# Where fifteen column sums are scaled, and how the second-last row is split: the tail of a row-sum kernel

## The chip, the cores and the metric

The kernel runs on one core of a Trainium2 chip. The metric is the device time of one execution in microseconds (us), the median of several runs; lower is better. Besides the timed runs there is one execution that the hardware profiler recorded, and all durations below are from it.

## The reference

The input is 32 x 512 x 1024 numbers in float32 (64 MiB). Every row of 1024 is summed and divided by 1024:

```python
def reference(x: np.ndarray, divisor: float) -> np.ndarray:
    return (np.sum(x, axis=-1) / divisor).astype(np.float32)
```

So 67 MB are read and 64 KB are written; there are 16384 row sums.

## The kernel before

The 16384 rows are laid over 128 partitions, 128 rows in each. A partition's first 112 rows (the main part) and its last 16 rows (the last part) lie in different stretches of the input and of the output, so that the main part's results can be stored while the last part is still being read. A "column" below is one of these rows seen from the result tiles: `res` holds 112 columns of finished sums, `q` and `fin` 16 each.

**The loads.** All loads are issued by SyncE (SP), in program order, on one DMA queue. The main part comes in pieces of 2, 14 (seven times) and 12 rows per partition, into three rotating buffers `t`. The last part comes as 8 rows (a fourth use of those buffers), then 4 and 2 rows in tiles of their own, then one row (`row`, lines 172 to 176), and then the very last row in three pieces: `pa` (columns 0 to 447), `pb` (448 to 703) and `pc` (704 to 1023), lines 180 to 186. Rows 8 + 4 + 2 are 14, so `j` is 14 at line 172: `row` is column 14 of the last part, and the three pieces are column 15.

**The sums.** Of each piece VectorE (DVE) sums most rows with one `reduce_sum` (line 153); in the pieces at the end ScalarE (ACT) sums some rows, one ACTIVATE each with an accumulator that a second instruction reads out (line 147). The single row `row` is split between the two engines: DVE sums its first 768 elements into `q[:, 14]` (line 176), ACT sums the other 256, already multiplied by 1/1024, into `r[:, 14]` (line 175). `r` is set to zero by a GpSimd (POOL) memset at the start (line 139), because line 194 reads fifteen columns of it.

**The tail.** ACT sums `pa` into an extra column of `pc` (line 192), DVE sums `pb` into a second extra column (line 193). Line 194 is one DVE instruction that makes `fin[:, 0:15]` as `q * scale + r`. Line 198 is one DVE instruction that multiplies `pc`, with its two extra columns, by 1/1024 and accumulates the result into `fin[:, 15]`; this too is followed by an instruction that reads the accumulator. Line 201 stores `fin`. Earlier, at line 189, POOL multiplies the 112 columns of `res` by 1/1024, and line 190 stores them.

**What sets the order.** The engines work through the program in its order; semaphores are set by the tile framework, by the regions of a tile that are written and read. Three functions edit the finished program. `start_loads_at_once` puts the first loads ahead of the start barrier. `latest_wait_first` orders an instruction's waits where it has several: the first stays on the instruction, the others go to small semaphore instructions ahead of it. `close_while_storing` moves the last store (line 201) behind SP's closing drain (line 232 in the profile), so that the other engines' closing barrier runs while the store is under way. SP's closing waits thus stand ahead of the last store: one for each load that is still out, for the landing of the store of `res`, and for the last work of POOL and ACT. The store itself then waits for DVE alone, and the program's end waits for the store's landing (line 88).

Of the kernel before, what the change touches and what calls it, by code (L numbers as in the profile page):

```python
# [9 lines left out]
F32 = mybir.dt.float32  # L10
ADD = mybir.AluOpType.add
MULT = mybir.AluOpType.mult
# [55 lines left out]
def close_while_storing(nc, landed):  # L68


    body, end = nc.main_func.blocks[1], nc.main_func.blocks[-1]
    store = [i for i in body.instructions if i.engine == SP and type(i).__name__ == "InstDMACopy"][-1]
    (lane,) = store.sync_info.on_update
    drain = end.instructions[0]
    assert drain.engine == SP and type(drain).__name__ == "InstDrain"
    needs = {w.id: w for w in drain.sync_info.on_wait}
    assert needs[lane.id].wait_value > lane.update_value
    needs[lane.id] = dataclasses.replace(
        needs[lane.id], wait_value=needs[lane.id].wait_value - lane.update_value
    )  # L80

    (done,) = [w for w in store.sync_info.on_wait if w.ant_name.startswith("DVE_")]
    assert needs[done.id].wait_value == done.wait_value
    del needs[done.id]
    own = dict(sync_type="semaphore", id=landed.num, ant_name=landed.name)
    add = mybir.SyncUpdate(update_mode="sem-add-imm", update_value=16, **own)
    sub = mybir.SyncUpdate(update_mode="sem-sub-imm", update_value=16, **own)
    last = nc.sync.wait_ge(landed, 16).ins
    assert nc.main_func.blocks[-1].instructions[-1].name == last.name
    body.instructions = [i for i in body.instructions if i.name != store.name]  # L90
    end.instructions = [
        with_sync(drain, on_wait=tuple(needs.values())),
        with_sync(store, on_wait=(done,), on_update=(add,)),
        *end.instructions[1:-1],
        with_sync(last, on_update=(sub,)),
    ]


@with_exitstack
def kernel(  # L100
    ctx: ExitStack,
    tc: tile.TileContext,
    x: bass.AP,
    divisor: float,
    out: bass.AP,
):
    nc = tc.nc
    landed = nc.alloc_semaphore("landed")
    nc.at_finalize(start_loads_at_once)
    nc.at_finalize(latest_wait_first)  # L110
    nc.at_finalize(lambda nc: close_while_storing(nc, landed))
    xf = x.flatten_outer_dims()
    N, D = xf.shape
    P = nc.NUM_PARTITIONS
    scale = 1.0 / float(divisor)
    J = N // P
    assert J * P == N


    L = 16  # L120
    M = J - L
    x_main = bass.AP(tensor=x.tensor, offset=0, ap=[[M * D, P], [D, M], [1, D]])
    x_last = bass.AP(tensor=x.tensor, offset=P * M * D, ap=[[L * D, P], [D, L], [1, D]])
    o_main = bass.AP(tensor=out.tensor, offset=0, ap=[[M, P], [1, M]])
    o_last = bass.AP(tensor=out.tensor, offset=P * M, ap=[[L, P], [1, L]])


    main = [(2, 0)] + [(14, 0)] * 6 + [(14, 4), (12, 5)]
    last = [(8, 4), (4, 2), (2, 1)]
    assert sum(n for n, _ in main) == M and sum(n for n, _ in last) == L - 2  # L130
    bulk = ctx.enter_context(tc.tile_pool(name="bulk", bufs=3))
    one = ctx.enter_context(tc.tile_pool(name="one", bufs=1))
    psum = ctx.enter_context(tc.tile_pool(name="junk", bufs=4, space=bass.MemoryType.PSUM))

    res = one.tile([P, M], F32, name="res")
    fin = one.tile([P, L], F32, name="fin")
    q = one.tile([P, L], F32, name="q")
    r = one.tile([P, L], F32, name="r")
    nc.gpsimd.memset(r, 0.0)  # L139

    def load(dst, src):
        tc.keep_in_program_order(nc.sync.dma_start(out=dst, in_=src))  # L142

    def act_sum(dst, src, by=1.0):
        n = src.shape[-1]
        junk = psum.tile([P, D], F32, name="junk")
        nc.scalar.activation(junk[:, :n], src, COPY, scale=by, accum_out=dst)  # L147

    def sums(dst, t, rows, on_act):
        d = rows - on_act  # L150
        for i in range(d, rows):
            act_sum(dst[:, i : i + 1], t[:, i, :])
        nc.vector.reduce_sum(out=dst[:, :d], in_=t[:, :d, :], axis=AX)  # L153

    j = 0
    for rows, on_act in main:
        t = bulk.tile([P, 14, D], F32, name="t")
        load(t[:, :rows, :], x_main[:, j : j + rows, :])
        sums(res[:, j : j + rows], t, rows, on_act)
        j += rows  # L160
    j = 0
    for rows, on_act in last:
        if rows == 8:
            t = bulk.tile([P, 14, D], F32, name="t")[:, :8, :]
        else:
            t = one.tile([P, rows, D], F32, name=f"t{rows}")
        load(t, x_last[:, j : j + rows, :])
        sums(q[:, j : j + rows], t, rows, on_act)
        j += rows


    c = 768
    row = one.tile([P, D], F32, name="row")
    load(row, x_last[:, j, :])
    act_sum(r[:, j : j + 1], row[:, c:], by=scale)
    nc.vector.reduce_sum(out=q[:, j : j + 1], in_=row[:, :c], axis=AX)  # L176

    a, b = 448, 704  # L180
    pa = one.tile([P, a], F32, name="pa")
    pb = one.tile([P, b - a], F32, name="pb")
    pc = one.tile([P, D - b + 2], F32, name="pc")
    load(pa, x_last[:, L - 1, :a])
    load(pb, x_last[:, L - 1, a:b])
    load(pc[:, : D - b], x_last[:, L - 1, b:])


    nc.gpsimd.tensor_scalar_mul(out=res, in0=res, scalar1=scale)  # L189
    tc.keep_in_program_order(nc.sync.dma_start(out=o_main, in_=res))  # L190

    act_sum(pc[:, D - b : D - b + 1], pa)
    nc.vector.reduce_sum(out=pc[:, D - b + 1 :], in_=pb, axis=AX)  # L193
    nc.vector.scalar_tensor_tensor(  # L194
        out=fin[:, : L - 1], in0=q[:, : L - 1], scalar=scale, in1=r[:, : L - 1], op0=MULT, op1=ADD
    )
    scaled = one.tile([P, D - b + 2], F32, name="scaled")
    nc.vector.tensor_scalar(  # L198
        out=scaled, in0=pc, scalar1=scale, scalar2=0.0, op0=MULT, op1=ADD, accum_out=fin[:, L - 1 :]
    )  # L200
    tc.keep_in_program_order(nc.sync.dma_start(out=o_last, in_=fin))
# [35 lines left out]
```

## Time and profile before

| | us |
|---|---|
| median of 4 runs | 161.35 (161.31 to 161.41) |
| the profiled execution: its own time | 161.32 |
| its span, first to last instruction | 159.8 |
| DVE busy | 121.1 (76%) |
| ACT busy | 19.6 (12%) |
| POOL busy | 0.8 |
| DMA: 67.18 MB | mean 420 GB/s over the span |

The span leaves out some 1.5 us of the profiled execution's time that lies around the program's instructions. The busy time of an engine is a mean over the whole span; the tail that the change touches is the last 4 us, and it is read from the views in order of time. "Landing" is when a DMA's last piece has signalled its semaphore.

The rows of the operations that the change touches: the memset of `r` took 112 ns, the DVE sum of `row` 954 ns for 768 columns, ACT's sum of the other 256 columns 388 ns and 187 ns to read the accumulator, line 194 on DVE 174 ns, and POOL's scaling of `res` (112 columns) 493 ns.

### The profile page before, as it was taken

Reading aid. Unit: us, or ns where it says so; the run is one execution under the profiler, and the core shown is the slowest. Engines: PE = TensorE matmul, PEld = TensorE weight load, DVE = VectorE, ACT = ScalarE, POOL = GpSimd, SP = SyncE. Lnnn points to the kernel's source line nnn. Section 1 sums busy time; section 2 is a strip of 40 time slices with the busy share of each in tenths; the row PEclk is TensorE's granted clock in tenths of the full one; section 3 lists DMA queues with packets and bytes.
Section 4 is the critical chain, followed back from the end, with each engine's and each line's share of the span. In section 5 each row is a group of like instructions: output and inputs, shape, how many; then the busy total and the mean of one; then the engine's idle time right before and its main releaser. Section 6 shows DMA issues by size and latency. Waiting matters only on the chain.

```text
span 159.8 us, 139 instructions
## 1 busy us (share of the span) xinstructions
DVE 121.1 (76%) x17; ACT 19.6 (12%) x37; POOL 0.8 (0%) x6
## 2 busy tenths in 40 slices
DVE  0500059995999599978999599959995996494985
ACT  3000000000000000000000000000000900480973
POOL 0000000000000000000000000000000000001000
DMA  7999999978999999969999999969999999899993
GB/s 248 474 459 459 459 459 459 445 316 388 459 459 459 459 459 459 445 302 402 459 459 459 459 459 459 445 273 431 459 459 427 394 468 517 361 427 390 402 410 128
DMA packets 2592, 67.18 MB, mean 420 GB/s; under 512 B 544, under 2 KB 928, under 8 KB 1056
## 3 DMA queue, kind: packets, MB, share of 16 engines
q1 hardware_dynamic: 2592, 67.18, 98.0%
HBM read 67.11 MB, written 0.07 MB: 420 GB/s over the span
## 4 chain that ended last, share of the span: by engine, by line
DMA 76%; DVE 22%; SPq 0%; issue 0%; DVEq 0%
DMA t<-in_x_dram 76%; DVE res L153 20%; DVE q L153 1%; DVE q L176 1%; SPq L142 0%; DVE scaled L198 0%; DVE pc L193 0%; DVE fin L194 0%; DVEq L198 0%; DVEq L232 0%
## 5 line engine op out<-in xcount | busy, mean ns | idle before, releaser
L153 DVE TENSOR_REDUCE res<-t 128x14 f32<-128x14336 f32 (+3 forms) x9 | 111.2, 12360 | 34.4 <-DMA t<-in_x_dram 34.4
L147 ACT ACTIVATE junk<-t 128x1024 f32<-128x1024 f32 x16 | 16.2, 1012 | 135.9 <-DMA t<-in_x_dram 135.9
L153 DVE TENSOR_REDUCE q<-t 128x4 f32<-128x4096 f32 (+2 forms) x3 | 7.9, 2642 | 2.7 <-DMA t<-in_x_dram 2.5
L147 ACT ACTIVATION_READ_ACCUMULATOR junk<-t 128x1 f32 x16 | 3.0, 187 | 0.0
L147 ACT ACT_TABLE_LOAD x1 | 1.3, 1283 | 1.7 <-PEq L218 1.7
L189 POOL TENSOR_SCALAR res<-res 128x112 f32<-128x112 f32 x1 | 0.5, 493 | 143.9 <-DVE res L153 143.9
L176 DVE TENSOR_REDUCE q<-row 128x1 f32<-128x768 f32 x1 | 1.0, 954 | 0.0
L198 DVE TENSOR_SCALAR_CACHE_REDUCE scaled<-pc 128x322 f32<-128x322 f32 x1 | 0.5, 489 | 0.1
L147 ACT ACTIVATE junk<-pa 128x448 f32<-128x448 f32 x1 | 0.5, 548 | 0.0
L193 DVE TENSOR_REDUCE pc<-pb 128x1 f32<-128x256 f32 x1 | 0.4, 411 | 0.0
L147 ACT ACTIVATE junk<-row 128x256 f32<-128x256 f32 x1 | 0.4, 388 | 0.1
L194 DVE SCALAR_TENSOR_TENSOR fin<-q,r 128x15 f32<-128x15 f32 x1 | 0.2, 174 | 0.0
L147 ACT ACTIVATION_READ_ACCUMULATOR junk<-row 128x1 f32 x1 | 0.2, 187 | 0.0
L147 ACT ACTIVATION_READ_ACCUMULATOR junk<-pa 128x1 f32 x1 | 0.2, 187 | 0.0
L139 POOL MEMSET r<- 128x16 f32 x1 | 0.1, 112 | 1.3 <-POOLq L218 1.3
L218 POOL MEMSET const-uint8-127<- 128x1 uint8 x1 | 0.1, 102 | 0.0
L218 POOL MEMSET const-bfloat16-1.0<- 128x1 bf16 x1 | 0.1, 101 | 0.0
L218 POOL MEMSET const-float32-0.0<- 128x1 f32 x1 | 0.1, 99 | 0.2 <-issue 0.2
L218 POOL MEMSET const-float32-1.0<- 128x1 f32 x1 | 0.1, 100 | 0.0
L198 DVE DVE_READ_ACCUMULATOR scaled<-pc 128x1 f32 x1 | 0.1, 81 | 0.0
## 6 DMA issues: line engine op xcount, KB each, us to landing
t<-in_x_dram SPq DMA_DIRECT2D x7, 7168.0 KB, 35.7
t<-in_x_dram SPq DMA_DIRECT2D x1, 6144.0 KB, 33.3
t<-in_x_dram SPq DMA_DIRECT2D x1, 4096.0 KB, 26.0
t<-in_x_dram SPq DMA_DIRECT2D x2, 1024.0 KB, 18.7
t<-in_x_dram SPq DMA_DIRECT2D x1, 2048.0 KB, 30.5
row<-in_x_dram SPq DMA_DIRECT2D x1, 512.0 KB, 33.2
pa<-in_x_dram SPq DMA_DIRECT2D x1, 224.0 KB, 33.3
pc<-in_x_dram SPq DMA_DIRECT2D x1, 160.0 KB, 33.1
```

The costliest lines, as they stand in the source:

```text
L139: nc.gpsimd.memset(r, 0.0)
L147: nc.scalar.activation(junk[:, :n], src, COPY, scale=by, accum_out=dst)
L153: nc.vector.reduce_sum(out=dst[:, :d], in_=t[:, :d, :], axis=AX)
L176: nc.vector.reduce_sum(out=q[:, j : j + 1], in_=row[:, :c], axis=AX)
L189: nc.gpsimd.tensor_scalar_mul(out=res, in0=res, scalar1=scale)
L193: nc.vector.reduce_sum(out=pc[:, D - b + 1 :], in_=pb, axis=AX)
L194: nc.vector.scalar_tensor_tensor(out=fin[:, : L - 1], in0=q[:, : L - 1], scalar=scale, in1=r[:, : L - 1], op0=MULT, op1=ADD)
L198: nc.vector.tensor_scalar(out=scaled, in0=pc, scalar1=scale, scalar2=0.0, op0=MULT, op1=ADD, accum_out=fin[:, L - 1 :])
L218: nc = _bacc.Bacc("TRN2", target_bir_lowering=False, num_devices=1)
```

## The change

The scaling of columns 0 to 14 of `fin` goes from one DVE instruction to two POOL instructions: one scales the fourteen columns of `q`, the other makes column 14 as `q * scale + r`, with `r` as a value for each partition. `r` is now one column wide (a view of a tile of 16 columns, as wide as the tile was before), so it needs no zeroing, and the memset goes. `row` is split 704 to 320 between DVE and ACT in place of 768 to 256. The pieces of the very last row (448, 256 and 320 columns) are the same before and after, and no tile changes its size.

```diff
     res = one.tile([P, M], F32, name="res")
     fin = one.tile([P, L], F32, name="fin")
     q = one.tile([P, L], F32, name="q")
-    r = one.tile([P, L], F32, name="r")
-    nc.gpsimd.memset(r, 0.0)
+
+    r = one.tile([P, 16], F32, name="r")[:, :1]
...
-    c = 768
+    c = 704
     row = one.tile([P, D], F32, name="row")
     load(row, x_last[:, j, :])
-    act_sum(r[:, j : j + 1], row[:, c:], by=scale)
+    act_sum(r, row[:, c:], by=scale)
     nc.vector.reduce_sum(out=q[:, j : j + 1], in_=row[:, :c], axis=AX)
...
     act_sum(pc[:, D - b : D - b + 1], pa)
     nc.vector.reduce_sum(out=pc[:, D - b + 1 :], in_=pb, axis=AX)
-    nc.vector.scalar_tensor_tensor(
-        out=fin[:, : L - 1], in0=q[:, : L - 1], scalar=scale, in1=r[:, : L - 1], op0=MULT, op1=ADD
+    nc.gpsimd.tensor_scalar_mul(out=fin[:, :j], in0=q[:, :j], scalar1=scale)
+    nc.gpsimd.tensor_scalar(
+        out=fin[:, j : j + 1], in0=q[:, j : j + 1], scalar1=scale, scalar2=r, op0=MULT, op1=ADD
     )
```

## The prediction

> **What bounds the kernel now.** I read first the page's chain of work that ended last, by line.
>
> ```profile
> DMA t<-in_x_dram 76%; DVE res L153 20%; DVE q L153 1%; DVE q L176 1%; SPq L142 0%; DVE scaled L198 0%; DVE pc L193 0%; DVE fin L194 0%; DVEq L198 0%; DVEq L232 0%
> ```
>
> The loads carry it. The change touches no load, so it can act only behind the last of them: on L176, L194, L193 and L198, some 2 us in all. Next, the end of the same chain in order of time (start, duration, what).
>
> ```profile
> 156.19 0.96 DVE q L176
> 157.16 0.02 issue
> 157.18 0.17 DVE fin L194
> 157.35 0.34 DVE pc L193
> 157.69 0.04 DVEq L198
> 157.73 0.06 issue
> 157.79 0.49 DVE scaled L198
> ```
>
> From 156.19 on, DVE works without a gap that matters, and its end releases the store. Two of these pieces change: L176 gets shorter, L194 goes. Then the timeline, for what lies beside them (start, duration, engine, line).
>
> ```profile
> 145.69 0.49 POOL L189 TENSOR_SCALAR res<-res 128x112 f32<-128x112 f32 x1 [143.85 <-DVE res L153]
> ...
> 156.19 0.39 ACT L147 ACTIVATE junk<-row 128x256 f32<-128x256 f32 x1
> ...
> 156.74 0.55 ACT L147 ACTIVATE junk<-pa 128x448 f32<-128x448 f32 x1
> 157.18 0.17 DVE L194 SCALAR_TENSOR_TENSOR fin<-q,r 128x15 f32<-128x15 f32 x1
> 157.22 0.19 ACT L147 ACTIVATION_READ_ACCUMULATOR junk<-pa 128x1 f32 x1
> 157.27 0.41 DVE L193 TENSOR_REDUCE pc<-pb 128x1 f32<-128x256 f32 x1
> ```
>
> POOL has been idle since 146.18. ACT has its last sum at 157.41. L193 starts at 157.27, before L194 has ended (157.18 + 0.17 = 157.35): independent DVE instructions overlap by 0.08. Last, SP's own waits and the DMAs' landings, because SP must pass its closing waits before it may issue the last store.
>
> ```profile
> SPq L232 <- DMA out_dram<-res: 0.6, 1, 0.6
> ...
> SPq L201 <- DVE scaled L198: 0.5, 1, 0.5
> ```
>
> ```profile
> row<-in_x_dram SPq DMA_DIRECT2D x1, 512.0 KB, 33.2
> pa<-in_x_dram SPq DMA_DIRECT2D x1, 224.0 KB, 33.3
> pc<-in_x_dram SPq DMA_DIRECT2D x1, 160.0 KB, 33.1
> pb<-in_x_dram SPq DMA_DIRECT2D x1, 128.0 KB, 33.1
> out_dram<-res SPq DMA_DIRECT2D x1, 56.0 KB, 11.5
> out_dram<-fin SPq DMA_DIRECT2D x1, 8.0 KB, 1.4
> ```
>
> With the issue times of the timeline (122.94, 123.42, 124.37, 123.89, 146.21, 158.32) the landings are: `row` 156.1, `pa` 156.7, `pc` 157.5, `pb` 157.0, the store of `res` 157.7, the last store 159.7. The span ends with that landing. SP is free of the `res` store at 157.7 and then stands 0.5 for DVE: that is the most that a faster tail can give before this store binds.
>
> **The change part by part.**
>
> *The memset of `r` goes* (112 ns at 1.72): POOL's next work is at 145.69. Worth nothing; 143 us of idle POOL hide it.
>
> *DVE's part of `row`, 768 to 704 columns.* Two DVE sums of one row give the slope: (954 - 411) ns / (768 - 256) = 1.06 ns per column, so 64 columns are 68 ns and L176 takes 0.89. It starts at 156.19 as before, on the landing of `row` (ACT starts on it in the same moment), and ends at 157.08.
>
> *ACT's part, 256 to 320 columns.* Slope (548 - 388) / (448 - 256) = 0.83 ns, so 53 ns more. The cover: ACT's sum of `pa` starts at 156.74 because `pa` lands at 156.7. The readout of `row` moves from 156.51 to 156.56; earlier ACTIVATEs start 0.09 behind such a readout's start (153.49 to 153.58), so ACT is ready by 156.65. Cost nothing; if the cover were gone, 0.05 on an engine that still has 0.1 to spare, see below.
>
> *L194 leaves DVE.* Its start to the start of L193 is 157.18 to 157.27, 0.09; before it, DVE waited 0.03 to 0.04 for its own sum to be written, which L193 needn't. So L193 can start at the end of L176 plus the old gap, 157.11, or, with the overlap of 0.08 that the pair L194, L193 shows, at 157.00. There `pb` stops it: it lands at 157.0 and starts follow a landing by 0.02 (154.94 to 154.96), so about 157.05. L193 starts at 157.05 to 157.11 in place of 157.27: 0.16 to 0.22 earlier.
>
> *What is late next for L198.* It starts 0.11 behind the end of L193 (157.68 to 157.79), now at 157.57 to 157.63. Its other inputs: ACT's sum of `pa`, 157.41 + the same 0.11 = 157.52, and `pc`, 157.5 + 0.02. Both are earlier, by 0.05 to 0.1. So the whole 0.16 to 0.22 arrives, and no more than 0.27 could.
>
> *Two instructions come on POOL, and with them a new wait of SP.* Both are the operation of L189 (TENSOR_SCALAR), with 14 columns and with one. Nothing shows them this small, or with a scalar read from memory: below, POOL's own 128x1 memsets take 0.10; above, L189 takes 0.49 for 112 columns. I take 0.49 for both, the only row of the operation. The first needs the 14 columns of `q`, ready at 154.96 + 1.22 = 156.18; POOL starts 0.09 behind DVE (145.60 to 145.69), so it runs 156.27 to 156.76, beside L176. The second needs L176, 157.08, and ACT's 320 columns, 156.75: it runs 157.17 to 157.66 (157.27 at the lower bound). Nothing is queued behind it on POOL but the closing drain, which nobody needs before SP's store has been issued. SP sees POOL 0.03 later (146.18 to 146.21), at 157.69: that is while SP still stands for the `res` store. DVE releases the last store at 158.32 - 0.2 = 158.12. The cover is thus 0.43 beyond the 0.49; I price the pair at nothing.
>
> The Trainium skill, "GPSIMD Engine Reference", section "When to use GPSIMD", speaks against such a move: elementwise work belongs on VectorE, GpSimd taking about twice as long. By that each would take 2 x 0.17 = 0.35 and still be hidden, so rule and trace disagree on the merit, not on the duration: the rule prices an engine, the chain prices a place in time.
>
> *The sum.* 159.76 - 0.20 in the span (the page's 159.8; the last store's 1.4 is unchanged), the profiled execution 161.32 - 0.20 = 161.12. The median shown is 0.03 above that execution; on its scale I forecast 161.14, 0.13% less. About 0.2% (0.32 us) is what a measurement of this kernel can tell from no change, so I call this "same".
>
> **The rivals.**
>
> *Nothing arrives (161.3 to 161.4).* A DMA sets the end: `pc` or the `res` store lands later than in this execution, or L193 is held by `pb`. For it: margins of 0.05 to 0.1 at L198 against landings that end one behind the other. Against: SP's 0.5 of waiting for DVE after the `res` store. A part loss would give 161.2.
>
> *POOL comes last (slower).* One mechanism: the one-column instruction, whose scalar comes from memory, takes long, and SP stands for it before the store. It decides from a duration of 158.12 - 157.17 - 0.03 = 0.92; the time before is reached at 1.12, and 0.2% more at 1.44. Its price: the longest first use of a function in this trace is ACT's table load, 1.28 us; with that on top of 0.49 POOL ends at 158.94, SP issues at 158.97, 0.65 late: 162.0. Against: L189 was POOL's first TENSOR_SCALAR, started 0.09 behind its input and took 0.49, with nothing of the kind to be seen. "GPSIMD Engine Reference", section "Instruction dispatch", has a first call to newly loaded code at about 6 us; that would make some 166, and L189's row shows none of it.
>
> *POOL and DVE hinder each other (slower).* In the profile POOL never runs beside DVE late (L189 lies in a gap of DVE from 145.60 to 147.69), so no row denies it. If DVE stood while POOL ran, 2 x 0.49 - 0.2 = 0.78 more: 162.1; a small part of this would just eat the gain.
>
> *More than forecast.* Only if `pa`'s sum and `pc` come earlier too, up to the `res` store's 0.5: 160.8.
>
> **How the numbers follow.** Forecast (161.05 to 161.25) 0.64; nothing or a part arrives 0.20, all of it within 0.2%; POOL last 0.07, hindrance 0.04, of which 0.03 together stay within 0.2% and 0.08 are slower; more than forecast 0.05, nearly all of it over 0.2%. So faster 0.05, same 0.87, slower 0.08. The range goes from 161.0 (a gain of 0.27 with the runs' scatter of 0.05) to 161.5 (nothing arrives, POOL at the start of its late side); the rest of POOL's upper bound (162.0, 162.1) is left out with some 0.1.
>
> **What would show it.** Right: L176 near 0.89; L193 starting 157.05 to 157.11, or as far behind `pb`'s landing as said; L198 starting 0.11 behind L193's end; the chain still ending with DVE L198 ahead of SP; POOL's second instruction over before SP has the `res` store. Wrong: SP's longest last wait naming POOL; L193 or L176 longer than 1.06 ns per column says, beside POOL; L198 released by ACT or by `pc`; L193 still starting 0.1 or more behind L176.

## The result and the profile after

| | before | after |
|---|---|---|
| median, us | 161.36 (52 runs, 161.21 to 161.78) | 161.13 (32 runs, 161.00 to 161.49) |
| the profiled execution, us | 161.32 | 161.18 |
| its span, us | 159.8 | 159.6 |
| start of L176, us into the span | 156.19 | 156.26 |
| start of the last DVE sum (L198, now L199) | 157.79 | 157.66 |
| issue of the last store | 158.32 | 158.19 |

The ratio is 0.9986, with a 95% interval of 0.9981 to 0.9991: 0.23 us less, between 0.15 and 0.31. It is a small gain, but its interval lies clear of 1: the 0.32 us that the prediction gave as the least that can be told from no change was too coarse for this many runs.

The end of the chain that ended last, in the changed kernel (start, duration, what):

```profile
156.26 0.89 DVE q L176
157.15 0.40 DVE pc L193
157.55 0.04 DVEq L199
157.59 0.08 issue
157.66 0.49 DVE scaled L199
```

Against before, the piece `DVE fin L194` is gone with the wait ahead of it, and L176 is 0.07 shorter. From the start of L176 to the start of the last DVE sum it was 157.79 - 156.19 = 1.60 us; now it is 157.66 - 156.26 = 1.40. That is the gain, 0.20. The two profiled executions differ by only 0.13 at the last store's issue, because the one of after started its tail 0.07 later: the piece of two rows before it landed at 155.01 in place of 154.94. Measured from the start of L176, both views say the same.

The timeline of the changed kernel beside this chain (start, duration, engine, line):

```profile
156.33 0.26 POOL L194 TENSOR_SCALAR fin<-q 128x14 f32<-128x14 f32 x1 [10.09 <-DVE q L153]
156.64 0.19 ACT L147 ACTIVATION_READ_ACCUMULATOR junk<-row 128x1 f32 x1
156.81 0.55 ACT L147 ACTIVATE junk<-pa 128x448 f32<-128x448 f32 x1
157.12 0.42 DVE L193 TENSOR_REDUCE pc<-pb 128x1 f32<-128x256 f32 x1
157.25 0.27 POOL L195 TENSOR_SCALAR fin<-q,r 128x1 f32<-128x1 f32 x1 [0.66 <-DVE q L176]
```

Both POOL instructions are there, 0.26 and 0.27 us long, and over at 157.52. L193 starts at 157.12, still 0.03 ahead of L176's end and 0.02 behind the landing of `pb`, which this trace has at 157.10 (before: at 157.03, 0.24 ahead of L193). ACT starts on `pa` 0.55 behind its start on `row` (156.26), as it did before (156.19 to 156.74), although its sum of `row` has grown from 388 to 442 ns. SP's own waits:

```profile
SPq L233 <- DMA out_dram<-res: 0.6, 1, 0.6
...
SPq L202 <- DVE scaled L199: 0.4, 1, 0.4
```

SP still waits for DVE last, 0.4 in place of 0.5, and no wait for POOL shows.

### The profile page after: what moved, and what is told of

Read it like the earlier page. It is cut to its first block, busy times and chain, and to the rows that moved or that the text cites. A ratio compares the mean times of both kernels' runs of the same rounds, so it can differ in the third digit from the quotient of the medians.

```text
span 159.6 us, 140 instructions
## 1 busy us (share of the span) xinstructions
DVE 120.9 (76%) x16; ACT 19.7 (12%) x37; POOL 1.2 (1%) x7
## 4 chain that ended last, share of the span: by engine, by line
DMA 76%; DVE 22%; SPq 0%; issue 0%; DVEq 0%
DMA t<-in_x_dram 76%; DVE res L153 20%; DVE q L153 1%; DVE q L176 1%; SPq L142 0%; DVE scaled L199 0%; DVE pc L193 0%; DVEq L199 0%; DVEq L233 0%
## 5 line engine op out<-in xcount | busy, mean ns | idle before, releaser
L153 DVE TENSOR_REDUCE res<-t 128x14 f32<-128x14336 f32 (+3 forms) x9 | 111.2, 12360 | 34.4 <-DMA t<-in_x_dram 34.4
L153 DVE TENSOR_REDUCE q<-t 128x4 f32<-128x4096 f32 (+2 forms) x3 | 7.9, 2642 | 2.7 <-DMA t<-in_x_dram 2.5
L189 POOL TENSOR_SCALAR res<-res 128x112 f32<-128x112 f32 x1 | 0.5, 496 | 145.3 <-DVE res L153 145.3
L176 DVE TENSOR_REDUCE q<-row 128x1 f32<-128x704 f32 x1 | 0.9, 885 | 0.0
L199 DVE TENSOR_SCALAR_CACHE_REDUCE scaled<-pc 128x322 f32<-128x322 f32 x1 | 0.5, 490 | 0.1
L193 DVE TENSOR_REDUCE pc<-pb 128x1 f32<-128x256 f32 x1 | 0.4, 420 | 0.0
L194 POOL TENSOR_SCALAR fin<-q 128x14 f32<-128x14 f32 x1 | 0.3, 262 | 10.1 <-DVE q L153 10.1
L199 DVE DVE_READ_ACCUMULATOR scaled<-pc 128x1 f32 x1 | 0.1, 82 | 0.0
```

The costliest lines, as they stand in the source:

```text
L194: nc.gpsimd.tensor_scalar_mul(out=fin[:, :j], in0=q[:, :j], scalar1=scale)
L199: nc.vector.tensor_scalar(out=scaled, in0=pc, scalar1=scale, scalar2=0.0, op0=MULT, op1=ADD, accum_out=fin[:, L - 1 :])
```

## The experiments

Two theories of the gain. *One:* the scaling of the fifteen columns leaves DVE; L193 then depends on nothing that DVE does just before, so it overlaps L176 and is released by the landing of `pb`; the new split of `row` adds next to nothing on top. *Two:* DVE's pieces simply add up, and each part of the change brings its share. Beside these stand the question how much cover POOL has, whether POOL and DVE hinder each other, and what the width of the tile `r` is for. All ratios are to the kernel before on the same chip, with 95% intervals; its median there was 161.29 (first eight runs) and 161.30 (last four).

**Only the move to POOL (e1)**

```diff
-    c = 704
+    c = 768
```

> Only the move to POOL: row stays split 768 to 256. Theory one (in the changed kernel L193 is released by the landing of pb, 0.02 before it started, and no longer by DVE): L193 overlaps L176 by 0.08 and starts 0.87 behind the start of L176, against 0.86 in the changed kernel and 1.08 before, so nearly the whole gain is there already: 0.18 to 0.20 us under before, about 161.16. Rival two (the parts add up by DVE's work, each 64 columns 0.07, no overlap): L193 starts 0.97 behind the start of L176, and the time is 0.13 under before, about 161.23.

Measured: 161.01 us, ratio 0.9990 (0.9978 to 1.0001). From its chain:

```profile
156.40 0.95 DVE q L176
157.35 0.34 DVE pc L193
```

The chain counts L193 only from the end of L176; the timeline has its start:

```profile
157.27 0.41 DVE L193 TENSOR_REDUCE pc<-pb 128x1 f32<-128x256 f32 x1
```

That is 0.87 behind L176, as theory one said (rival: 0.97). The last DVE sum starts at 157.80, 1.40 behind L176: the changed kernel's distance. In the trace, the move alone holds the whole 0.20. Which of the two limits stops L193 here, the overlap or the landing of `pb`, e1 can't say: it starts 0.08 ahead of L176's end, the overlap that the pair L194, L193 showed, and 0.03 behind `pb`, which landed at 157.24, so both fall together. In this profile `row` landed late (1.73 behind the piece of two rows, against 1.23 in the changed kernel); the profiled execution, 161.32 us, is slower than most of e1's runs, but the distances above count from L176's start, behind that landing. The timed runs can't tell e1 from the changed kernel, nor, with an interval that includes 1, from the kernel before: that the move alone is enough rests on the trace.

**Only the split (e2)**

```diff
 (the kernel before)
-    c = 768
+    c = 704
```

> Only the split 704 to 320, L194 stays on DVE with its 15 columns, and r with its memset. Both theories: L176 takes 0.89, L194 and L193 start 0.07 earlier relative to the start of L176 (L193 at 1.01 behind it, still well behind the landing of pb), and 0.07 us is gained, about 161.29. If the 320 columns on ACT held L194, less than that; ACT should be done 0.33 before L194 starts.

Measured: 161.15 us, ratio 0.9996 (0.9985 to 1.0006). L193 starts at 157.39, 1.01 behind L176 (156.38), and the last DVE sum at 157.92, 1.54 behind it, against 1.60 before: 0.06. The mechanism is as expected; by the time alone it is not to be told from nothing. So, by the traces, the parts do not add: 0.20 by the move, 0.06 by the split, 0.20 by both. (In five more profiles of kernels with both parts, e5, e6, e8, e9 and e10, the distance is 1.38 to 1.41; the sum of the parts would be 1.34.)

**The split taken further (e3)**

```diff
-    c = 704
+    c = 640
```

> The changed kernel with row split 640 to 384, so 64 columns less on DVE again. Theory one (pb's landing releases L193): nothing more is gained, L193 starts 0.02 behind pb's landing as before, 161.13. Rival two (DVE's work in L176 bounds L193): 0.07 more, 161.06. ACT's sum of pa should still start at pa's landing; if it doesn't, L199 comes up to 0.03 later.

Measured: 161.03 us, ratio 0.9984 (0.9975 to 0.9992). Its chain no longer runs through L176 at all:

```profile
123.80 33.21 DMA pb<-in_x_dram
157.00 0.03 issue
157.03 0.43 DVE pc L193
```

L176 ran from 156.07 for 0.82 and was over at 156.89; L193 waited for `pb`, which landed at 157.00, and started 0.03 behind it. Sixty-four columns less on DVE bring nothing once `pb` is the later one. ACT began on `pa` at 156.70, 0.03 behind the landing of `pa`, so the 384 columns did not hold it either.

**Smaller `pb`, larger `pc` (e4)**

```diff
-    c = 704
+    c = 640
-    a, b = 448, 704
+    a, b = 448, 672
```

> The changed kernel with row split 640 to 384 and the last row cut 448, 224, 352 in place of 448, 256, 320. Theory one: pb lands about 0.04 earlier and L193 takes 0.39, so it ends 0.07 earlier; then ACT's sum of pa (0.06 ahead of L193's end in the changed kernel) is the last input of L199, which takes 0.03 longer: 0.02 to 0.04 us under the changed kernel, 161.10. Rival (pc's landing or the store of res bounds L199 and the last store already): 0.03 over it, 161.16.

Measured: 161.15 us, ratio 0.9988 (0.9978 to 0.9999). From its chain:

```profile
124.25 33.32 DMA pc<-in_x_dram
157.57 0.04 issue
157.61 0.52 DVE scaled L199
```

L193 ended at 157.48 as hoped, but then `pc`'s landing released the last sum, as the rival had it, not ACT, whose sum of `pa` was over at 157.45. Cut this way, `pc` starts 128 bytes off a multiple of 256, in the input and in its tile (the runs on the width of `r` below show why that could matter); it landed 1.34 behind `row`, within the 1.25 to 1.44 of the other runs with the tiles in place, so nothing shows that its place made it late. The sum starts 1.35 behind L176, 0.05 less than in the changed kernel, and lasts 0.03 longer. What is left is below what these runs can measure. In the changed kernel the three inputs of the last DVE sum come so close together that a cut elsewhere only changes which is last.

**More POOL work, first try (e5 with one instruction, e6 with three; the diff is that of e5)**

```diff
+    spare = one.tile([P, M], F32, name="spare")
+    for _ in range(1):
+        nc.gpsimd.tensor_scalar_mul(out=spare, in0=res, scalar1=scale)
     tc.keep_in_program_order(nc.sync.dma_start(out=o_last, in_=fin))
```

> The changed kernel with one more POOL instruction behind the two: 112 columns of res scaled into a spare tile, which nobody reads (added work alone). It took 0.50 as L189, so POOL ends near 158.0 in place of 157.52. Theory (POOL has cover until DVE releases the last store, 158.16): no change, 161.13. Rival (POOL's end was already close to the path, by SP's closing wait or by POOL's closing drain): up to 0.4 more, 161.5.

> The same with three more such POOL instructions (added work alone). They end at 157.52 plus 3 times 0.50, near 159.0, if they don't overlap; SP's closing wait for POOL is then the last, and the store goes 0.8 later than in the changed kernel: 161.9 or so, less if POOL's instructions overlap (0.26 of each was its fixed part). Were SP not held by POOL at all: 161.13.

Measured: 161.20 (0.9993, 0.9984 to 1.0002) and 161.15 (0.9988, 0.9979 to 0.9997). Neither says anything on POOL's cover. The timeline has the added instructions right behind L189, from 146.28 and from 146.17: they read only `res`, so the framework's scheduler placed them there, 10 us ahead of the tail. They are of use as two more measurements of the changed kernel.

**More POOL work, behind the two (e9 with one, e10 with three; the diff is that of e9)**

```diff
+    spare = one.tile([P, M], F32, name="spare")
+    for _ in range(1):
+        nc.gpsimd.tensor_scalar(
+            out=spare, in0=res, scalar1=scale, scalar2=fin[:, j : j + 1], op0=MULT, op1=ADD
+        )
     tc.keep_in_program_order(nc.sync.dma_start(out=o_last, in_=fin))
```

> The changed kernel with one more POOL instruction (added work alone) that has column 14 of fin as its scalar, so that it can only run behind the change's two: 112 columns of res into a spare tile that nobody reads. By the 40 instructions of the run before this form takes about 0.27 for one column and 1.49 for 512, so some 0.53 for 112: POOL ends near 158.1, just ahead of DVE's release of the last store, 158.16. Theory (POOL has cover until then): no change, 161.13 to 161.2. Rival (POOL's end counts earlier, in SP's closing waits or by its drain): 0.3 to 0.5 more.

> The same with three (added work alone). POOL ends near 157.52 + 3 x 0.55, about 159.2. Theory (SP's closing wait for POOL stands ahead of the last store): the store is issued 0.03 behind POOL's end, some 1.0 later than in the changed kernel, 162.2 or so, and SP's last wait names POOL in place of DVE. Rival (the store waits for DVE alone, and POOL only for the end of the program): the barrier ends some 0.9 later than it did, past the store's landing by 0.6 at most, 161.7.

Measured: with one, 161.20 us, ratio 0.9992 (0.9983 to 1.0002); with three, 161.94 us, ratio 1.0036 (1.0023 to 1.0049). SP's own waits, with one:

```profile
SPq L238 <- POOL spare L204: 0.2, 1, 0.2
...
SPq L207 <- DVE scaled L199: 0.2, 1, 0.2
```

and with three:

```profile
SPq L238 <- POOL spare L204: 1.1, 1, 1.1
```

The timeline with three has

```profile
157.64 1.27 POOL L204 TENSOR_SCALAR spare<-res,fin 128x112 f32<-128x112 f32 x3
159.00 0.34 SPq L207 DMA_DIRECT2D out_dram<-fin  x1
```

With one, the added instruction runs from 157.69 for 0.36. SP now stands 0.2 for POOL and then 0.2 for DVE: the wait for POOL has eaten half of the wait for DVE, and the store goes out no later. With three, POOL is over at 157.64 + 1.27 = 158.91, SP waits for POOL alone, and the store is issued at 159.00, where DVE (157.68 + 0.49) would have let it go at 158.2. So POOL is on the path from the point at which DVE releases the store, and not before. The size I gave was wrong: three took 1.27, not 1.65, and the time is 161.94, not 162.2.

**POOL beside DVE (e8)**

```diff
+    spare = one.tile([P, 512], F32, name="spare")
+    nc.gpsimd.memset(spare, 1.0)
+    for k in range(40):
+        if k % 2:
+            nc.gpsimd.tensor_scalar_mul(out=spare, in0=spare, scalar1=scale)
+        else:
+            nc.gpsimd.tensor_scalar(
+                out=spare, in0=spare, scalar1=scale, scalar2=spare[:, :1], op0=MULT, op1=ADD
+            )
```

> The changed kernel with 40 POOL instructions of the change's two kinds, of 512 columns each, on a tile of its own from the start on (added work alone), so that POOL runs beside several of DVE's 14-row sums. Theory (they don't hinder each other): the 14-row sums stay at 15.09 us each and the time is within 0.1 of the changed kernel. Rival (a shared way to the memory): sums that lie beside POOL take measurably longer, up to POOL's busy time.

Measured: one run, 161.32 us. That is 0.14 over the changed kernel's profiled execution, more than the 0.1 expected, but the span is 159.6 in both, so the difference lies outside the program's instructions, and it is a single time. Busy time by stretch, each stretch one 14-row sum of DVE (us, DVE, ACT, POOL, clock, DMA share, GB/s):

```profile
21.83:36.92 15.09, 15.09 (x1) 0.00 (x0) 13.89 (x14) 1.00 0.98 426
38.77:53.86 15.09, 15.09 (x1) 0.00 (x0) 10.06 (x9) 1.00 0.98 426
55.72:70.81 15.09, 15.09 (x1) 0.00 (x0) 0.00 (x0) 1.00 0.98 426
```

The sum takes 15.09 with POOL busy for 13.89 of it, for 10.06 of it, and idle; the DMA moves 426 GB/s in all three. There is no hindrance between these POOL instructions and this DVE reduction. The Trainium skill, "GPSIMD Engine Reference", section "Specifications", says that the two share an interface to the memory and clash where DVE runs in a mode with two ports or has two inputs in it; L153, L176 and L193 have one input, and the trace agrees with the rule as far as it goes: no run here has POOL beside a DVE instruction with two inputs.

**The width of the tile `r` (e7, e11 and e12: one of the three lines each)**

```diff
-    r = one.tile([P, 16], F32, name="r")[:, :1]
+    r = one.tile([P, 1], F32, name="r")
+    r = one.tile([P, 32], F32, name="r")[:, :1]
+    r = one.tile([P, 24], F32, name="r")[:, :1]
```

> The changed kernel with r as a tile of one column (a smaller tile) in place of a view of a tile of 16, so that the tiles allocated behind it start on other addresses, by less than 64 bytes, and the loads of the last part land there. Theory: the DMA's rate doesn't change, no difference, 161.13. Rival (writes that aren't on 64-byte boundaries cost the loads time): the last loads land later and the time is over 161.3.

> The changed kernel with r as a view of a tile of 32 columns (a larger tile): everything behind it lies 64 bytes further on. Theory (multiples of 64 bytes are alike for the loads): as the changed kernel, 161.13. Rival (any other place costs): 161.4 to 161.5 as with the tile of one column.

> The changed kernel with r as a view of a tile of 24 columns (a larger tile): everything behind it lies 32 bytes further on, and r's own form, a view, stays. Theory (a place 32 bytes off 64 costs the last loads time): as with the tile of one column, 161.4 to 161.5, with the loads of 4 and 2 rows and of row each landing 0.06 or more later behind the one before. Rival (it was the tile of one column itself, or chance): 161.13.

`r` is allocated ahead of the tiles of the last loads (4 rows, 2 rows, `row`, `pa`, `pb`, `pc`). With 16 columns, 64 bytes, all six start on multiples of 256 bytes in the built program; the three variants shift them by -32, +64 and +32 bytes. In e8 the spare tile of 512 columns stands between `r` and them and shifts them by 2048 bytes, a multiple of 256: a control that was not planned as one.

| `r` | shift, bytes | median (all runs) | ratio | 4 rows | 2 rows | `row` | `pa` |
|---|---|---|---|---|---|---|---|
| changed kernel | 0 | 161.13 (161.00 to 161.49) | 0.9986 (0.9981 to 0.9991) | 4.84 | 2.43 | 1.23 | 0.55 |
| e9, POOL work behind | 0 | 161.20 (161.03 to 161.65) | 0.9992 (0.9983 to 1.0002) | 4.82 | 2.43 | 1.25 | 0.53 |
| e8, POOL work beside | +2048 | 161.32 (one run) | | 4.85 | 2.43 | 1.22 | 0.55 |
| e7 | -32 | 161.47 (161.34 to 161.71) | 1.0008 (0.9999 to 1.0017) | 4.90 | 2.50 | 1.64 | 0.61 |
| e11 | +64 | 161.40 (161.33 to 161.64) | 1.0008 (0.9999 to 1.0016) | 4.89 | 2.51 | 1.28 | 0.63 |
| e12 | +32 | 161.39 (161.37 to 161.46) | 1.0003 (0.9994 to 1.0012) | 4.91 | 2.50 | 1.29 | 0.62 |

The last four columns are the distances, in us, from ACT's start on one piece to its start on the next; ACT starts on the landing of each. All three shifted kernels have these loads later behind the one before, by 0.05 to 0.1 in the pieces of 4 and 2 rows and in `pa`, by 0.03 to 0.06 in `row` (e7's `row`, 0.4 later, is not put down to the place: with the tiles in place `row` came 1.73 behind in e1 and 1.49 in e4). In e8, moved by a multiple of 256, they are not later. `pc` alone is no later behind `pb` in the three, 0.41 to 0.44 from landing to landing against 0.39 to 0.49 with the tiles in place. From issue to landing, the last loads of e11:

```profile
row<-in_x_dram SPq DMA_DIRECT2D x1, 512.0 KB, 33.4
pa<-in_x_dram SPq DMA_DIRECT2D x1, 224.0 KB, 33.5
pc<-in_x_dram SPq DMA_DIRECT2D x1, 160.0 KB, 33.3
pb<-in_x_dram SPq DMA_DIRECT2D x1, 128.0 KB, 33.4
```

Each is 0.2 to 0.3 over the same line of before. That is the loss in the medians too: 161.39 to 161.47 against 161.15 to 161.20 for kernels on the same chips with the tiles in place (e5, e6, e9). The intervals of the ratios overlap, so it is the landings that carry this reading. My theory for e11, that multiples of 64 bytes are alike, fell; so did the rival of e12, that it was `r`'s own form.

## Why the prediction was right, point by point

- **L176, 0.89 by the slope of 1.06 ns per column.** Measured 885 ns.
- **L193, 0.86 to 0.92 behind the start of L176** (157.05 to 157.11 against 156.19). Measured 0.86: the lower end, which rested on the overlap of 0.08 that the pair L194, L193 had shown, with `pb`'s landing as the stop. The overlap is seen with `pb` long landed in the kernel before and in e2, `pb` as the stop by itself in e3; in e1 the two fall together.
- **The last DVE sum, 0.11 behind L193's end, 0.16 to 0.22 earlier.** Measured 0.12 behind an L193 that took 0.42 in place of 0.41: 0.20 earlier. The forecast was 161.12 on the profiled execution's scale and 161.14 on the median's; measured 161.18 and 161.13. The first is high by 0.06, about the 0.07 by which that execution's loads landed later.
- **ACT's longer sum costs nothing.** 442 ns, and `pa` is still started on its landing.
- **The two POOL instructions, priced at nothing.** Right in place, wrong in size: 0.26 and 0.27 where I took 0.49, the row of 112 columns. At 157.52 they were over before the store of `res` landed (157.7). The doubling that the prediction took from the Trainium skill, "GPSIMD Engine Reference", section "When to use GPSIMD", is given there for operations with two inputs; these have one, column 14 a scalar for each partition beside it, and took about 1.5 times L194's 0.17.
- **The split of `row`.** The steps were right, but the prediction did not draw out what they said of the split: with L194 gone, L193 is stopped by the landing of `pb` and starts 0.02 behind it, and most of the 64 columns' 0.07 has nowhere to go. e1 shows that the move alone reaches the same 1.40, e2 that the split is worth 0.06 only while L194 still stands behind it.
- **The rival "nothing arrives".** Not what happened, but the thin margins it named are real: in e4 `pc`'s landing releases the last sum.
- **The rival "POOL comes last".** It needed 0.92 us in POOL's second instruction, which took 0.27. e9 and e10 show the mechanism where the prediction put it, at SP's closing wait.
- **The rival "POOL and DVE hinder each other".** Not seen with POOL busy for 13.89 of 15.09 us (e8), nor in L176, 885 ns beside POOL's first instruction as the slope says. L193, beside the second, took 420 ns in place of 411, by a hair one of the signs of being wrong that the prediction named; with 414 in e1, also beside POOL, and 415 in e2 without, the 9 ns stay unexplained.

Left open: whether the tiles of the last loads must start on multiples of 256 bytes or 128 would do (no run had 128 for all of them; the buffers `t` lie 128 off in every kernel here, so nothing compares them), why the shifted loads land later, and the slow `row` in the profiles of e1, e4 and e7. No version was found that is faster than the changed kernel by more than the runs scatter.

## What to carry to other kernels

When two engines and several loads meet at one last instruction, write down when each input comes: a part taken off one of them is worth only the distance to the next, so parts don't add (0.20 and 0.06 made 0.20). Work for an idle engine is priced by its place, not by its speed: POOL was free until DVE released the store, and cost its full excess from there on. A tile that changes its width moves all that is allocated behind it, so look at where the targets of the last loads start.

## What the runs showed of the hardware

- Independent DVE instructions overlap: L193 starts 0.08 ahead of the end of L194 in the kernel before (157.27 against 157.35) and in e2 (157.39 against 157.30 + 0.17), with `pb` long landed, while a sum that reads the result of the one before starts 0.11 to 0.12 behind its end.
- POOL's TENSOR_SCALAR takes 0.26 for 14 columns and 0.27 for one with a scalar from memory; with 512 columns (e8) 0.69 with one operation and 1.49 with two and a scalar from memory. So at one or fourteen columns the width hardly counts, and at 512 the form does. At 112 columns the order is turned round: 0.49 with one operation (L189, e5), 0.36 with two and a scalar from memory (e9). The cause is open.
- Loads of 0.13 to 2 MB into tiles shifted by 32 or 64 bytes off a multiple of 256 land 0.03 to 0.1 us later each (`pc` excepted), 0.2 to 0.3 over the tail, for -32, +32 and +64 alike. The Trainium skill, "DMA: Bandwidth & Descriptors", section "How a descriptor splits into AXI transactions", has transactions start only at multiples of 256 bytes, so that a descriptor that starts elsewhere can cost more. But it speaks of what is read; here the places that are read stayed as they were and only the tiles that are written moved, of which the section says nothing. So it does not explain the loss, and it gives no time for it.
